# High halves first in three places, and a third gate projection ahead of the state-space outputs

## Chip, core and metric

The kernel runs on one core of a Trainium2 chip. The metric is device time in microseconds, the median of three runs. TensorE (PE) does the matmuls, VectorE (DVE) and ScalarE (ACT) everything elementwise, GpSimd (POOL) and SyncE (SP) little but memory sets and DMA issues.

## What is computed

One layer of a bidirectional hybrid encoder on 1024 tokens of width 1024, in float32. Three mixers (a state-space model S5, a gated linear recurrence RG-LRU, a gated linear attention GLA) work on slices of one projection; each is projected up, multiplied by its gate and added; a mixing matrix, a residual and a mixture of 16 experts follow.

```python
def reference(x, ...):
    h = x
    xn = rms_norm(h, mix_norm_g)
    p = xn @ w_in
    y_s5 = s5_mixer(p[..., OFF_S5:OFF_LRU], ...)
    y_lru = rg_lru_mixer(p[..., OFF_LRU:OFF_Q], ...)
    y_gla = gla_mixer(p[..., OFF_Q:OFF_K], p[..., OFF_K:OFF_V], ...)
    gates = jax.nn.sigmoid(p[..., OFF_GATE:].reshape(bsz, seq, N_BRANCH, D_MODEL))
    merged = (gates[:, :, 0] * (y_s5 @ w_up_s5)
              + gates[:, :, 1] * (y_lru @ w_up_lru)
              + gates[:, :, 2] * (y_gla @ w_up_gla))
    h = h + merged @ w_mix_out
    h = h + ec_ffn(rms_norm(h, ffn_norm_g), w_router, w_exp_gate, w_exp_up, w_exp_down)
    return rms_norm(h, final_norm_g)

def rg_lru_direction(xc, w_a, b_a, w_x, b_x, lam, reverse):
    xr = xc.reshape(bsz, seq, LRU_BLOCKS, LRU_BLOCK)
    r = jax.nn.sigmoid(jnp.einsum('bsnc,ncd->bsnd', xr, w_a).reshape(bsz, seq, LRU_WIDTH) + b_a)
    i = jax.nn.sigmoid(jnp.einsum('bsnc,ncd->bsnd', xr, w_x).reshape(bsz, seq, LRU_WIDTH) + b_x)
    log_a = -LRU_C * r * jax.nn.softplus(-lam)
    a = jnp.exp(log_a)
    mult = jnp.sqrt(jnp.maximum(-jnp.expm1(2 * log_a), 0))
    _, h = lax.associative_scan(_lin_combine, (a, mult * (i * xc)), reverse=reverse, axis=1)
    return h
```

## The kernel before

Every float32 product is made of three matmuls. An operand is split into a high half, rounded by a copy on ACT (L54), and a low half, the difference, taken on DVE (L62, or L57 where a scale goes in); a product is then high·low + high·high + low·high, accumulated in one PSUM tile. `mm3` (L67) writes these three in that order, with the low half of its last argument first. `wsplit` loads weights (`wraw`) and splits them into `wh` and `wl`.

All matmuls in question are 128x128 by 128x512. `proj` (matmuls at L386) makes one 128-column block of the input projection from the normalized input (xnH, xnL): 8 chunks x 3 products x 2 halves of the tokens are 48 matmuls into a PSUM tile `pj`, of which there are two. `gate` calls it for a gate block and evacuates with tanh on ACT. `up` (L396) multiplies a mixer's output halves y with a block of its up-projection: 12 matmuls for S5 and GLA, 24 for the LRU. `gated` joins both on DVE and adds to `merged`.

The stages are Python generators. `drive` takes a list of tasks (projections, gates with ups) and a generator, and after every task goes some steps on in the generator; when the tasks are out, the generator runs to its end alone:

```python
    def drive(tasks, gen, n):
        for t in tasks:
            t()
            for _ in range(n):
                next(gen, None)
        for _ in gen:
            pass
```

A scheduler then orders the instructions of each engine, with a preference for what stands in `tc.high_priority()`, and the buffer counts of the pools set how far ahead it can go. Each engine works its own list in order.

Until 272 us the S5 generator runs, with the remaining columns of the projection and two gates of branch 0 (`early_gate`, pool `pgp` of two buffers) as tasks. Then `s5_out(0)` and `s5_out(1)` use these two: gate, up, `gated`. In the GLA stage (to 447 us) the tasks are `s5_out(2)` to `s5_out(7)`, each of which makes its own gate, and `ahead(0)` to `ahead(2)`, three gates for later (`gates_s5`, L849). The generator computes two head pairs: scores (L789), masked on DVE (L795), products with the values (L802, L809), a normalization and eight transposes (L835), and y. In the LRU stage (to 565 us) the tasks are `gla_out` and the gates of its branch. For each of four channels, a convolution gives xc, its halves are xch and xcl (L62), and 24 matmuls (`mm3` in `lru_gen`, L925, profile lines L68 to L70) make the gates r and i in both directions, into `mx` tiles, of which there are four; scans on DVE (L950) follow. The rest of the gates and ups run until 688 us, and then the mixer: eight token tiles, each of 24 matmuls of the halves of merged (MH, ML) with the mixing weights (wmh, wml) into a bank `mo`, of which there are two; `residual` empties it on DVE (H). Experts follow from 835 us on.

Of the kernel before, what the change touches and what calls it, by code (L numbers as in the profile page):

```python
# [20 lines left out]
KT = D // P  # L21
# [21 lines left out]
def hybrid_encoder(ctx: ExitStack, tc: tile.TileContext, A, out, dbg=None):  # L43
# [346 lines left out]
    def up(w, ys, j):  # L390
        wh, wl = wsplit(w[:, j * P:(j + 1) * P], len(ys))
        ps = pj()
        for k, (yh, yl) in enumerate(ys):
            for i, (ww, yy) in enumerate(((wh, yl), (wh, yh), (wl, yh))):
                for h in range(2):
                    te.matmul(ps[:, h], ww[:, k], yy[:, h * 512:(h + 1) * 512],  # L396
                              start=(k == 0 and i == 0), stop=(k == len(ys) - 1 and i == 2))
        return ps
# [64 lines left out]
    def early_gate(j):  # L463
        if not early:
            early[-1] = pgctx.enter_context(tc.tile_pool(name="pgp", bufs=2, side="left", reuse_waits="tile"))
        early[j] = gate(0, j, early[-1])
# [23 lines left out]
    cols_rest += [lambda j=j: evac(proj(O_LRU + j * P), LD[j * P:(j + 1) * P]) for j in range(4)]  # L490
    cols_rest += [lambda j=j: early_gate(j) for j in range(2)]

# [187 lines left out]

    for j in range(2):
        s5_out(j)
# [165 lines left out]

    gates_s5 = [lambda j=j: s5_out(j) for j in range(2, KT)] + [lambda j=j: ahead(j) for j in range(3)]  # L849
    drive(gates_s5, gla_gen(), 10)  # L850
# [60 lines left out]
    def lru_gen():  # L911
        for c in range(4):
# [3 lines left out]
            for d in range(2):  # L916
# [4 lines left out]
                for h in range(2):  # L921
                    hs = slice(h * 512, h * 512 + 512)
                    for i, (o_, hb_) in enumerate(((rr_, hba), (ii_, hbx))):
                        ps = mx()
                        mm3(ps, WGh[:, 2 * d + i], WGl[:, 2 * d + i], xh[:, hs], xl[:, hs], True, True)  # L925
                        act(o_[:, hs], ps, AF.Tanh, bias=hb_[:, q], scale=0.5)
# [160 lines left out]
    PT = psm.tile([P, 2, 512], F32, name="PT", bufs=1)  # L1087

    def mix(t, w, ps, k0, k1):
        for k in range(k0, k1):  # L1090
            mm3(ps, MH[t][:, k], ML[t][:, k], w[0][:, k], w[1][:, k], k == 0, k == KT - 1)
# [25 lines left out]
    for t in range(NT):  # L1117
        ps = bank("mo")
        mix(t, wm[0], ps, 0, 2)
        next(lgen, None)  # L1120
        mix(t, wm[0], ps, 2, 4)
        next(lgen, None)
        mix(t, wm[0], ps, 4, KT)
        residual(t, 0, h0, ps, w0p)
# [563 lines left out]
```

## Time and profile before

| what | us |
| --- | --- |
| median of 3 runs | 1964.01 |
| lowest and highest | 1962.24, 1964.66 |
| profiled run, its time | 1962.37 |
| its span, first to last instruction | 1960.3 |

The granted clock of TensorE, mean over the profiled run, is 0.983. The profile was read in this way: the busy times by stretch, then what PE waits for, then the timeline at the places that the change touches. A row of the timeline is a start, a duration, the engine, the line, what is written from what, a count, and in brackets the idle time of the engine just before with what ended it.

### The profile page before, as it was taken

To read this page: it belongs to the slowest core of one execution; us is meant where nothing else is said; L and a number is where in the kernel's file an instruction comes from. 1 tells how busy PE (TensorE), PEld (TensorE's weight loads), DVE (VectorE), ACT (ScalarE), POOL (GpSimd) and SP (SyncE) were. 2 spreads that over 40 slices of the span, in tenths; PEclk is the share of its full clock that TensorE was granted. 3 is DMA by queue.
4 is the path that set the end of the run, shared out by engine and by line. 5 is a ranking of instruction groups with operands and counts; after the bars stand their busy time and mean duration, and the time that the engine had idled before them with its cause. 6 is when DMAs were issued, how large, how long until landed. Compare 5 with 4: busy or idle time off the path is not lost.

```text
span 1960.3 us, 25359 instructions
## 1 busy us (share of the span) xinstructions
PE 1871.1 (95%) x9502; PEld 1536.3 (78%) x9502; DVE 1499.6 (76%) x1896; ACT 1167.0 (60%) x1381; POOL 150.9 (8%) x207
## 2 busy tenths in 40 slices
PE   7999999999899999489999999999999999999996
PEld 6878866777778878368888888888888888888884
DVE  6467225558874253889999999999999999999987
ACT  5221234435672131357778777777777877777785
POOL 1834000000000001000000000000000000000000
PEclk9999999999999999689999999999999999999998
DMA  5431331302213163779999999999999999999992
GB/s 170 107 101 38 97 98 29 87 25 72 70 34 88 33 225 127 303 284 370 390 386 383 391 379 378 384 389 384 384 390 379 379 383 394 379 383 388 385 356 97
DMA packets 263231, 495.94 MB, mean 253 GB/s; under 512 B 26757, under 2 KB 82469, under 8 KB 263109
## 3 DMA queue, kind: packets, MB, share of 16 engines
q1 hardware_dynamic: 253476, 466.54, 65.3%
q0 software_dynamic: 7184, 25.69, 4.3%
q10 hardware_dynamic: 2448, 2.10, 0.5%
q8 instruction: 74, 1.21, 0.2%
q14 instruction: 49, 0.39, 0.1%
HBM read 464.55 MB, written 29.74 MB: 252 GB/s over the span
## 4 chain that ended last, share of the span: by engine, by line
PE 80%; DVE 6%; ACT 2%; issue 2%; DMA 1%; SPq 0%; POOLq 0%; DVEq 0%; ACTq 0%
PE py L1484 17%; PE pj L386 13%; PE gu L68 12%; PE gu L70 12%; PE gu L69 12%; PE pj L396 3%; PE tp L1441 2%; PE mo L68 2%; PE mo L70 2%; PE mo L69 2%; ACT xwh L54 1%; DVE junk L1342 1%; DVE lr L950 1%; PE mx L809 0%; PE mx L802 0%
## 5 line engine op out<-in xcount | busy, mean ns | idle before, releaser
L239 DVE TENSOR_TENSOR xwl<-rawb,xwh 128x1024 fp32r<-128x1024 f32 x528 | 613.8, 1218 | 40.0 <-ACT xwh L54 39.1
L54 ACT ACTIVATE xwh<-rawb 128x1024 fp32r<-128x1024 f32 x528 | 521.7, 1052 | 14.1 <-PE gu L70 7.4
L68 PE MATMUL gu<-xwl,xeh 128*128 128x512 f32 x1024 | 406.9, 397 | 0.0
L70 PE MATMUL gu<-xwh,xel 128*128 128x512 f32 x1024 | 399.8, 390 | 0.0
L69 PE MATMUL gu<-xwh,xeh 128*128 128x512 f32 x1024 | 399.0, 390 | 0.0
L239 DVE TENSOR_TENSOR xwl<-rawa,xwh 128x1024 fp32r<-128x1024 f32 x192 | 226.1, 1219 | 25.3 <-ACT xwh L54 25.3
L70 PEld LDWEIGHTS gu<-xwh,xel 128*128 128x128 f32 x1024 | 192.4, 188 | 41.5 <-DVE xel L62 0.2
L69 PEld LDWEIGHTS gu<-xwh,xeh 128*128 128x128 f32 x1024 | 192.8, 188 | 37.7
L68 PEld LDWEIGHTS gu<-xwl,xeh 128*128 128x128 f32 x1024 | 192.7, 188 | 37.3 <-ACT xeh L54 0.2
L54 ACT ACTIVATE xwh<-rawa 128x1024 fp32r<-128x1024 f32 x192 | 192.9, 1052 | 7.1 <-PE py L1484 7.1
L386 PE MATMUL pj<-xnL,wh 128*128 128x512 f32 x576 | 181.6, 394 | 3.9 <-ACT ev L54 2.2
L386 PE MATMUL pj<-xnH,wl 128*128 128x512 f32 x576 | 180.6, 393 | 0.0
L386 PE MATMUL pj<-xnH,wh 128*128 128x512 f32 x576 | 180.2, 392 | 0.0
L1484 PE MATMUL py<-xwl,hTh 128*128 128x512 f32 x512 | 159.2, 392 | 3.6 <-DVE xwl L239 3.6
L1484 PE MATMUL py<-xwh,hTl 128*128 128x512 f32 x512 | 158.0, 390 | 0.5 <-DVE hTl L62 0.5
L1484 PE MATMUL py<-xwh,hTh 128*128 128x512 f32 x512 | 157.8, 389 | 0.0
L54 ACT ACTIVATE wh<-wraw 128x1024 fp32r<-128x1024 f32 (+2 forms) x60 | 49.4, 827 | 176.8 <-PE pj L386 117.0
L62 DVE TENSOR_TENSOR wl<-wraw,wh 128x1024 fp32r<-128x1024 f32 (+2 forms) x60 | 57.6, 961 | 106.8 <-ACT wh L54 96.8
L386 PEld LDWEIGHTS pj<-xnL,wh 128*128 128x128 f32 x576 | 107.1, 188 | 30.4 <-ACT ev L54 3.7
L386 PEld LDWEIGHTS pj<-xnH,wh 128*128 128x128 f32 x576 | 107.9, 188 | 24.7 <-issue 2.0
L386 PEld LDWEIGHTS pj<-xnH,wl 128*128 128x128 f32 x576 | 107.2, 188 | 25.3 <-issue 1.9
L54 ACT ACTIVATE hTh<-tp 128x512 fp32r<-128x512 f32 x64 | 38.4, 599 | 125.3 <-PE tp L1441 125.3
(474 smaller groups left out, 2523.2 us busy)
## 6 DMA issues: line engine op xcount, KB each, us to landing
rawb<-in_w_exp_down_dram SPq DMA_DIRECT2D x90, 1024.0 KB, 8.8
rawb<-in_w_exp_up_dram SPq DMA_DIRECT2D x88, 1024.0 KB, 8.1
rawb<-in_w_exp_gate_dram SPq DMA_DIRECT2D x86, 1024.0 KB, 8.3
rawa<-in_w_exp_up_dram SPq DMA_DIRECT2D x40, 1024.0 KB
rawa<-in_w_exp_gate_dram SPq DMA_DIRECT2D x33, 1024.0 KB
rawa<-in_w_exp_down_dram SPq DMA_DIRECT2D x23, 1024.0 KB
wraw<-in_w_in_dram SPq DMA_DIRECT2D x36, 512.0 KB, 4.3
rawc<-in_w_exp_down_dram SPq DMA_DIRECT2D x15, 1024.0 KB
```

Of the source, the lines that this page charges most:

```text
L54: return s.activation(o, i, f, bias=bias, scale=scale, **k)
L62: (eng or v).tensor_tensor(lo, src, h.bitcast(F32), SUB)
L68: te.matmul(ps, lh, rl, start=first, stop=False)
L69: te.matmul(ps, lh, rh, start=False, stop=False)
L70: te.matmul(ps, ll, rh, start=False, stop=last)
L239: e.tensor_tensor(o, a, b, op)
L386: te.matmul(ps[:, h], w[:, k], xx[:, k, h * 512:(h + 1) * 512], start=(k == 0 and i == 0), stop=(k == KT - 1 and i == 2))
L396: te.matmul(ps[:, h], ww[:, k], yy[:, h * 512:(h + 1) * 512], start=(k == 0 and i == 0), stop=(k == len(ys) - 1 and i == 2))
L950: v.tensor_tensor_scan(rv(hh[d]), rv(hh[d]), rv(gi[d]), initial=0.0, op0=MUL, op1=ADD)
L1342: v.tensor_scalar(junk[:, half_], PT[:, half_], cand.bitcast(F32), 0.0, op0=OP.is_ge, op1=ADD, accum_out=cnt)
L1441: te.transpose(ps[:, j * P:(j + 1) * P], src[:, j * P:(j + 1) * P], idn)
L1484: te.matmul(E.py[:, h], a[:, j], b[:, h * 512:(h + 1) * 512], start=(f == 0 and j == 0 and p_ == 0), stop=(f == 3 and j == 3 and p_ == 2))
```

## The change

Four things. `up` takes the products with the high halves of all y first, then those with the low halves. `early_gate` makes three gates instead of two, with a third buffer, `s5_out(2)` moves in front of the GLA stage with it, and `gates_s5` has one task fewer. The LRU gates take WGh·xh and WGl·xh before WGh·xl. The first mixer tile takes its 16 products with MH before the 8 with ML, without the steps of `logits` in between (there are none at that point).

```diff
     def up(w, ys, j):
         wh, wl = wsplit(w[:, j * P:(j + 1) * P], len(ys))
         ps = pj()
-        for k, (yh, yl) in enumerate(ys):
-            for i, (ww, yy) in enumerate(((wh, yl), (wh, yh), (wl, yh))):
-                for h in range(2):
-                    te.matmul(ps[:, h], ww[:, k], yy[:, h * 512:(h + 1) * 512],
-                              start=(k == 0 and i == 0), stop=(k == len(ys) - 1 and i == 2))
+        terms = [(w_, k, y[0]) for k, y in enumerate(ys) for w_ in (wh, wl)] + [(wh, k, y[1]) for k, y in enumerate(ys)]
+        for i, (ww, k, yy) in enumerate(terms):
+            for h in range(2):
+                te.matmul(ps[:, h], ww[:, k], yy[:, h * 512:(h + 1) * 512], start=(i == 0), stop=(i == len(terms) - 1))
         return ps
...
-            early[-1] = pgctx.enter_context(tc.tile_pool(name="pgp", bufs=2, side="left", reuse_waits="tile"))
+            early[-1] = pgctx.enter_context(tc.tile_pool(name="pgp", bufs=3, side="left", reuse_waits="tile"))
...
-    cols_rest += [lambda j=j: early_gate(j) for j in range(2)]
+    cols_rest += [lambda j=j: early_gate(j) for j in range(3)]
...
-    for j in range(2):
+    for j in range(3):
         s5_out(j)
     pgctx.close()
...
-    gates_s5 = [lambda j=j: s5_out(j) for j in range(2, KT)] + [lambda j=j: ahead(j) for j in range(3)]
+    gates_s5 = [lambda j=j: s5_out(j) for j in range(3, KT)] + [lambda j=j: ahead(j) for j in range(3)]
     drive(gates_s5, gla_gen(), 10)
...
                         ps = mx()
-                        mm3(ps, WGh[:, 2 * d + i], WGl[:, 2 * d + i], xh[:, hs], xl[:, hs], True, True)
+                        gate_ = 2 * d + i
+                        for n, (w_, x_) in enumerate(((WGh, xh), (WGl, xh), (WGh, xl))):
+                            te.matmul(ps, w_[:, gate_], x_[:, hs], start=(n == 0), stop=(n == 2))
...
+    def mix_low_last(t, w, ps):
+        for k in range(KT):
+            te.matmul(ps, MH[t][:, k], w[0][:, k], start=(k == 0), stop=False)
+            te.matmul(ps, MH[t][:, k], w[1][:, k], start=False, stop=False)
+        for k in range(KT):
+            te.matmul(ps, ML[t][:, k], w[0][:, k], start=False, stop=(k == KT - 1))
+
...
-        mix(t, wm[0], ps, 0, 2)
-        next(lgen, None)
-        mix(t, wm[0], ps, 2, 4)
-        next(lgen, None)
-        mix(t, wm[0], ps, 4, KT)
+        if t:
+            mix(t, wm[0], ps, 0, 2)
+            next(lgen, None)
+            mix(t, wm[0], ps, 2, 4)
+            next(lgen, None)
+            mix(t, wm[0], ps, 4, KT)
+        else:
+            mix_low_last(t, wm[0], ps)
```

In the three places below, L386 rows are gate matmuls and L396 rows ups. Lines of the changed kernel are one lower around them, apart from L926, the LRU gates.

First PE at the end of the S5 stage, between the last products of its output gate (Z,wg) and the first up. Before:

```order
L386 MATMUL pj<-xnL,wh 128x512 x2
L644 MATMUL mx<-Z,wg 128x512 x8
L386 MATMUL pj<-xnH,wh 128x512 x2
L386 MATMUL pj<-xnH,wl 128x512 x2
L396 MATMUL pj<-y,wh 128x512 x4
L396 MATMUL pj<-y,wl 128x512 x2
```

and now:

```order
L643 MATMUL mx<-Z,wg 128x512 x8
L386 MATMUL pj<-xnH,wh 128x512
L386 MATMUL pj<-xnH,wl 128x512 x2
L386 MATMUL pj<-xnL,wh 128x512 x2
...
L386 MATMUL pj<-xnH,wh 128x512 x2
L386 MATMUL pj<-xnH,wl 128x512 x2
L396 MATMUL pj<-y,wh 128x512 x2
L396 MATMUL pj<-y,wl 128x512 x2
L396 MATMUL pj<-y,wh 128x512 x2
```

Four gate matmuls stood there, and 45 stand there now.

Second, PE at the end of the GLA stage, from the last scores of the second head pair to its transposes (idn,gt) and the first up of y. Before, the scores and the filling behind them:

```order
L789 MATMUL mx<-gin 128x128 x2
L386 MATMUL pj<-xnH,wl 128x512
L386 MATMUL pj<-xnL,wh 128x512 x2
L386 MATMUL pj<-xnH,wh 128x512 x2
L386 MATMUL pj<-xnH,wl 128x512
L802 MATMUL mx<-gt,sc 128x64
```

and further on, around the transposes:

```order
L386 MATMUL pj<-xnL,wh 128x512 x2
L386 MATMUL pj<-xnH,wh 128x512 x2
L386 MATMUL pj<-xnH,wl 128x512 x2
L835 MATMUL mx<-idn,gt 128x128 x8
L386 MATMUL pj<-xnL,wh 128x512 x2
L386 MATMUL pj<-xnH,wh 128x512 x2
```

and now:

```order
L788 MATMUL mx<-gin 128x128 x2
L801 MATMUL mx<-gt,sc 128x64
L808 MATMUL mx<-gt 64x64 x2
...
L801 MATMUL mx<-gt,sc 128x64 x2
L808 MATMUL mx<-gt 64x64 x4
L808 MATMUL mx<-gt,gin 64x64 x2
L834 MATMUL mx<-idn,gt 128x128 x8
L396 MATMUL pj<-y,wh 128x512 x2
L396 MATMUL pj<-y,wl 128x512 x2
```

No gate matmul stands there any more; before, there were six between the scores and the masked products, 25 between the last products and the transposes and twelve between these and the first up.

Third, PE at the LRU gates of the first channel. Before:

```order
L386 MATMUL pj<-xnH,wl 128x512
L68 MATMUL mx<-xcl,lwh 128x512
L69 MATMUL mx<-xch,lwh 128x512
L70 MATMUL mx<-xch,lwl 128x512
L68 MATMUL mx<-xcl,lwh 128x512
```

and now:

```order
L396 MATMUL pj<-y,wh 128x512
L926 MATMUL mx<-xch,lwh 128x512
L926 MATMUL mx<-xch,lwl 128x512
L926 MATMUL mx<-xch,lwh 128x512
L926 MATMUL mx<-xch,lwl 128x512
L926 MATMUL mx<-xch,lwh 128x512
L926 MATMUL mx<-xcl,lwh 128x512 x2
```

The products with xcl, first before, stand behind those with xch of several tiles now.

## Rows read from the trace of the kernel before

**Rows 1.** The head of the page.

```profile
span 1960.3 us, 25359 instructions
```

**Rows 2.** Busy time by stretch: PE, PEld, DVE, ACT, POOL, granted clock, DMA share, GB/s.

```profile
447.00:565.00 118.00, 109.55 (x464) 86.87 (x463) 101.27 (x116) 75.43 (x94) 0.54 (x8) 0.99 0.25 68
565.00:688.00 123.00, 123.00 (x543) 101.72 (x542) 48.83 (x47) 40.91 (x49) 1.04 (x11) 1.00 0.18 52
...
835.00:1940.00 1105.00, 1093.78 (x5108) 905.17 (x5108) 1011.94 (x994) 861.81 (x956) 43.19 (x33) 0.99 0.99 370
```

**Rows 3.** PE's waits to 800 us: total us, times, longest.

```profile
PE mx L68 <- DVE xcl L62: 5.5, 3, 2.5
...
PE pj L396 <- DVE y L57: 3.3, 2, 2.1
...
PE mo L70 <- DVE ML L57: 2.0, 1, 2.0
```

**Rows 4.** Timeline of PE at the S5 ups.

```profile
254.82 5.74 PE L644 MATMUL mx<-Z,wg 128*128 128x512 f32 x13
...
263.61 2.07 PE L396 MATMUL pj<-y,wh 128*128 128x512 f32 x4 [2.13 <-DVE y L57]
...
269.37 1.19 PE L396 MATMUL pj<-y,wh 128*128 128x512 f32 x4 [1.15 <-DVE y L57]
```

**Rows 5.** Timeline of PE in a gate, the first and the last of seven consecutive pairs.

```profile
239.03 0.61 PE L386 MATMUL pj<-xnH,wl 128*128 128x512 f32 x2
...
241.75 0.61 PE L386 MATMUL pj<-xnH,wl 128*128 128x512 f32 x2
```

**Rows 6.** Short stretches behind PE waits, columns as in rows 2.

```profile
263.50:266.50 3.00, 2.89 (x7) 2.31 (x8) 1.52 (x3) 1.38 (x1) 0.00 (x0) 0.52 0.19 49
266.50:269.30 2.80, 1.72 (x7) 1.06 (x5) 2.07 (x1) 0.70 (x1) 0.00 (x0) 0.90 0.00 0
528.60:531.60 3.00, 2.93 (x9) 2.36 (x10) 3.00 (x4) 1.82 (x3) 0.00 (x0) 0.71 0.00 0
531.60:534.00 2.40, 2.40 (x8) 1.88 (x7) 2.40 (x4) 1.81 (x4) 0.00 (x0) 0.65 0.30 51
690.80:694.00 3.20, 3.15 (x14) 2.57 (x15) 3.08 (x11) 2.28 (x4) 0.00 (x0) 1.00 1.05 406
```

**Rows 7.** Timeline at the end of the GLA stage.

```profile
432.25 0.39 PE L789 MATMUL mx<-gin 64*128 64x128 f32 x4
...
434.07 0.33 PE L802 MATMUL mx<-gt,sc 128*128 128x64 f32 x2
...
436.08 0.30 PE L809 MATMUL mx<-gt,gin 64*64 64x64 f32 x4
...
442.76 1.09 PE L835 MATMUL mx<-idn,gt 128*128 128x128 f32 x8 [0.49 <-DVE gt L239]
...
445.40 1.06 ACT L54 ACTIVATE y<-gt 128x1024 fp32r<-128x1024 f32 x1 [6.97 <-DVE gt L57]
...
446.47 1.07 PE L396 MATMUL pj<-y,wh 128*128 128x512 f32 x4
```

**Rows 8.** Timeline at the gates of the second LRU channel, and of the last.

```profile
495.64 1.06 ACT L54 ACTIVATE xch<-xc 128x1024 fp32r<-128x1024 f32 x1 [5.83 <-DVE xc L57]
497.66 1.20 DVE L62 TENSOR_TENSOR xcl<-xc,xch 128x1024 fp32r<-128x1024 f32 x1
...
498.92 0.50 PE L68 MATMUL mx<-xcl,lwh 128*128 128x512 f32 x1 [1.35 <-DVE xcl L62]
...
561.46 0.50 PE L68 MATMUL mx<-xcl,lwh 128*128 128x512 f32 x1 [1.65 <-DVE xcl L62]
```

**Rows 9.** Timeline of the mixer's beginning.

```profile
693.13 8.04 DVE L57 SCALAR_TENSOR_TENSOR ML<-merged,MH 128x1024 fp32r<-128x1024 f32 x7
...
701.08 1.49 DVE L239 TENSOR_TENSOR H<-mo,H 128x512 f32<-128x512 f32 x2
...
702.23 0.48 PE L68 MATMUL mo<-wml,MH 128*128 128x512 f32 x1
```

## The prediction

> **What bounds the kernel now.** I read the page's head first, for the span of 1960.3 us [rows 1], and then the busy times by stretch [rows 2]. From 835 us on, the experts hold TensorE (PE) for 1093.78 of 1105.00 us at a granted clock of 0.99. Nothing of that is touched, so whatever the front part gains or loses should reach the end at full size. In the front two kinds of stretch stand out. From 565 to 688 us PE is busy for 123.00 of 123.00 us: there only the number of matmuls counts. From 447 to 565 us, the RG-LRU stage, PE is busy for 109.55 of 118.00 us and VectorE (DVE) for 101.27: there a chain over DVE, ScalarE (ACT) and PE and the matmuls that fill PE's pauses are nearly equal, so removing a PE wait need not shorten anything.
>
> Next come PE's waits by what ended them, over the first 800 us [rows 3]. Three of the groups are the change's targets: the LRU gates wait 5.5 us for the low half of the convolved input (xcl) in three places, the up projections 3.3 us for a low half of y in two, the mixer 2.0 us for a low half (ML) in one. The timeline of PE then shows where: the S5 up projections after 2.13 us of idle at 263.61 and after 1.15 us at 269.37 [rows 4]. Last I read one stretch in which PE waits hardly at all, the end of the GLA stage [rows 7], because the order of the changed kernel takes the filling work from just there.
>
> **A unit of cost.** Every gate projection is 48 matmuls of 128x512. From the pair at 239.03 us to the pair at 241.75 lie six pairs, twelve matmuls, in 2.72 us [rows 5], which is 0.227 us each. So a gate costs 10.9 us of PE, wherever it stands; the change only moves it.
>
> **The change part by part.**
>
> *The third early gate and the S5 up projections: -5.0 us.* The order of the changed kernel has 45 gate matmuls between the last Z,wg products and the first up, 4 before. The Z,wg group ends near 260.5 us [rows 4], and 45 x 0.227 = 10.2 us of matmuls bring PE to about 270 to 271; the first up then begins with the high half of y, and the last low half is there at about 269.3, as the wait ending at 269.37 says. Both waits go: 2.13 + 1.15 = 3.28 us. There is more: behind the first wait the granted clock was 0.52 for 3.00 us and 0.90 for 2.80 us [rows 6], a loss of 3.00 x 0.48 + 2.80 x 0.10 = 1.7 us against full clock, which goes with it. Bounds: -3.3 (the clock falls elsewhere) to -5.0; I take -5.0, since PE then has matmuls through the whole tail. The high-first order in the ups adds nothing here, since the gate already covers both halves. The gate's own evacuation on ACT and the split of its weights (wh on ACT, wl on DVE) are the same instructions as before, earlier, and the first low half of y, there at 263.6, is wanted only at 270, so some microseconds are to spare.
>
> *The same gate is then missing in the GLA stage: +13.7 us.* The S5 gates are handed out one task at a time between steps of the GLA generator, and now there is one task fewer. In the order of the changed kernel the fillers are used up before the end. Counting gate and up matmuls in both orders: at the first transpose of the second head pair PE has done 1104 of them instead of 1041, that is 63 more (48 of the moved gate and 15 others pulled forward): +63 x 0.227 = +14.3 us. From there to the first GLA up projection the order holds 104 instead of 159, 55 fewer (12.5 us), but does the stretch become shorter? That is the main question, and the timeline answers it [rows 7]. From the last score product at 432.25 us to the masked product at 434.07 PE waits for two masking copies on DVE; the six gate matmuls between only fill that. From the end of the last output products (436.08 + 0.30) on, a chain runs outside PE: ACT squares, then DVE's reduction and reciprocal root, transposes on PE at 442.76, scaling, y on ACT at 445.40, the first up at 446.47. That is 10.1 us, during which PE now does 37 gate matmuls (37 x 0.227 = 8.4 us) and eight transposes (1.1 us). At 442.76 PE had already waited 0.49 us for DVE: the chain ends last there, not the filling. With the filling gone, the chain stays and PE idles: some 9 us at the end and 1.4 us in each of two mask steps, with smaller pieces of 0.5 and 1.1 us, which is about 12 to 13 us, the size of the work that left. What the stretch can lose is only the bit by which fillers held the chain up; at the transposes it is nothing, as the 0.49 us say, and the up at 446.47 starts at y's end (445.40 + 1.06), so again nothing. For the two mask steps, where the chain may have come a matmul's pitch or so later in each, I take -0.6, an estimate. Bounds: -0.6 to -12.5 (all of it, the rival below). So y of GLA is ready 14.3 - 0.6 - 5.0 = 8.7 us later than before.
>
> *The LRU gates, high halves first: +0.2 us.* In the channel at 498.92 us the high half is ready at 496.70 (495.64 + 1.06), the low half at 498.86, and PE waits 1.35 us for that [rows 8]. Now PE can run eight products (four PSUM banks, two products each) ahead of the low half: 8 x 0.227 = 1.8 us of work moved into the wait. But in front of the gates there is also less to do: by y of GLA the changed order has done 1208 gate and up matmuls (1200 before), by the last channel's gates 1569 (1578 before). The wait that remains is for the same instruction of DVE, xcl, which still stands behind the same scans; in the channel with the longest wait, 2.5 us [rows 3], DVE's order is unchanged. Since PE is full from 565 us on [rows 2], the stage's length is told by the last channel's gates and what is left then: 1.8 us less for the products done ahead, 9 matmuls more (2.0 us): +0.2. Bounds: the waits go altogether (-5.5), with them the low clock of 0.71 and 0.65 behind the 2.5 us wait [rows 6] (3.00 x 0.29 + 2.40 x 0.35 = -1.7) and the 8 matmuls done before y (-1.8), in all -9.0; the other end is the 2.0 us for 9 matmuls with nothing gained and one more stretch at the low clock, 1.7 us, in all +3.7. I take +0.2, nearest to the row at 561.46, where after 1.65 us of wait the PE-bound stretch begins.
>
> *The first mixer tile: 0.* It no longer waits 2.0 us. But its result sits in one of two banks (mo), and the tile after next needs that bank. The low halves of the other seven tiles occupy DVE from 693.13 for 8.04 us, and the addition that empties the first bank follows at 701.08; the third tile starts at 702.23 [rows 9]. DVE's order there is as before, so PE arrives 2 us earlier and waits 2 us longer, once. Bounds: -2.0 (other work fits) to +1.7 (the wait lowers the clock as the one of 2.13 us did).
>
> The Trainium skill, "Perfetto Trace Analysis", section "Optimizing Tensor Performance", asks that independent matmul groups rotate through PSUM banks so that one's evacuation overlaps the next group's matmuls. By that rule the tile's wait would be hidden and the gain of 2 us real; the rows speak against it here, since the evacuation stands behind DVE's splits.
>
> **Sum.** -5.0 + 14.3 - 0.6 + 0.2 + 0 = +8.9 us on the profiled run of 1962.37 us: 1971.3 us. The median of the runs is 1964.01, 1.6 us above the profiled run, so the forecast is **1972.9 us**. About 0.2%, or 3.9 us, is what a measurement of this kernel can tell from no change.
>
> **Rivals.**
>
> *The LRU stage pays it back* (0.16). If what bounds 447 to 565 us is PE's idle time and not the DVE chain, the term there is -9.0 instead of +0.2, and the sum -0.3; with the mixer's 2 us, -2.3. That gives 1961.7 to 1963.7 us, no change. For it: PE is busier than DVE there. Against: DVE turns to xcl at 497.66, a microsecond after the high half is there [rows 8], since other work stands ahead of it in its queue, and that work stays.
>
> *Faster: the GLA tail costs nothing* (0.08). If the fillers are what makes the chain late, the stretch shrinks by the whole 12.5 us that leave it. This decides as soon as the chain from 436.38 to 446.47 can run in what PE still has there, 1.1 us of transposes; the sum is then -5.0 + 14.3 - 12.5 + 0.2 = -3.0, and with the LRU term -12.2: 1951.8 to 1961.0 us. Against it stands the 0.49 us wait, and that no PE filler lies between most of the chain's steps.
>
> *The clock falls in each new pause* (0.15). Behind idles of 2.13 and 2.5 us the granted clock fell; after the mixer's 2.0 us it stayed at 1.00 [rows 3, 6]. The changed kernel has pauses of 6 and 3 us around the GLA transposes and perhaps one in the LRU stage and one in the mixer. At 1.7 us each, three of them give 1978.0 us. The Trainium skill, "TensorE: Matmul & The Clock Gate", section "HAM oscillation — how this bites in real kernels", describes this, a cold restart behind waits between bursts; the trace agrees at 0.52 and 0.71. I keep it as a rival because behind the GLA tail DVE's chain covers part of the slower matmuls.
>
> **How the numbers follow.** Forecast 0.61, the LRU stage pays back 0.16, faster tail 0.08, low clock 0.15. The forecast's own range is 1968 to 1977. The range reaches down over most of the first rival and up to the third: 1962.5 to 1978.0. Faster by over 0.2%: 0.08. Within 0.2%: 0.17, the first rival and a little of the forecast's lower edge, less what of the second rival falls there. Slower by over 0.2%: 0.75.
>
> **What would show it.** In the profile after: no PE wait ahead of the S5 ups, and full clock there; PE waits of about 6 and 3 us on either side of the second head pair's transposes and of 1.4 us before the last masked products; y of GLA about 8.7 us later; waits for xcl still there or replaced; a PE wait of about 2 us before the third mixer tile. If y of GLA is not later, the step on the filling is wrong; if it is later but the mixer begins on time, the LRU term is.

## The result: 0.7% slower

| kernel | median us | runs | lowest, highest | profiled run | its span |
| --- | --- | --- | --- | --- | --- |
| before | 1964.08 | 4 | 1962.24, 1964.66 | 1962.37 | 1960.3 |
| changed | 1978.09 | 4 | 1975.83, 1980.02 | 1980.02 | 1977.9 |

The ratio of after to before is 1.0068, 95% interval 1.0055 to 1.0081: 14.0 us slower between the medians, where the forecast was 8.9 slower. The median lies 0.1 us above the stated range, 1962.5 to 1978.0 us (the forecast's own part of it was 1968 to 1977). The four runs of the changed kernel stand in two pairs, near 1976 and near 1980; the profiled one is of the upper pair, 17.6 us above the profiled run of before.

PE's waits over the first 860 us, as in [rows 3] (total us, times, longest):

```profile
PE mx L834 <- DVE gt L239: 6.6, 2, 6.4
...
PE pj L386 <- ACT wh L54: 3.6, 2, 2.0
PE mx L801 <- DVE sc L794: 3.2, 5, 1.2
...
PE pt L1105 <- DVE H L239: 2.0, 1, 2.0
PE pj L396 <- ACT y L54: 1.9, 1, 1.9
...
PE mx L926 <- ACT xch L54: 1.7, 1, 1.7
PE mx L926 <- DVE xcl L62: 1.3, 1, 1.3
```

The wait of the S5 ups for y and the mixer's wait for ML are gone from the list, and the LRU gates wait 3.0 us in two places instead of 5.5 in three (a new wait of 2.0 us for split weights, wh, also lies in the LRU stage). In their place stand a wait of 6.4 us ahead of the second head pair's transposes (L834), 1.9 us ahead of the first GLA up, 1.2 us ahead of masked products (L801) and 2.0 us in the mixer (L1105). The changed kernel's timeline of PE at the places that [rows 4] and [rows 7] to [rows 9] show of before:

```profile
272.22 0.62 PE L396 MATMUL pj<-y,wh 128*128 128x512 f32 x2
...
371.70 1.06 PE L834 MATMUL mx<-idn,gt 128*128 128x128 f32 x8 [0.20 <-DVE gt L239]
...
432.82 0.43 PE L801 MATMUL mx<-gt,sc 128*128 128x64 f32 x2 [0.16 <-DVE sc L794]
...
439.26 0.69 PE L801 MATMUL mx<-gt,sc 128*128 128x64 f32 x2 [1.19 <-DVE sc L794]
...
446.68 0.69 PE L801 MATMUL mx<-gt,sc 128*128 128x64 f32 x2 [1.19 <-DVE sc L794]
...
457.31 1.97 PE L834 MATMUL mx<-idn,gt 128*128 128x128 f32 x8 [6.39 <-DVE gt L239]
461.21 1.22 PE L396 MATMUL pj<-y,wh 128*128 128x512 f32 x2 [1.93 <-ACT y L54]
...
574.38 0.39 PE L926 MATMUL mx<-xch,lwh 128*128 128x512 f32 x1
...
703.08 0.39 PE L1092 MATMUL mo<-wmh,MH 128*128 128x512 f32 x1
...
716.66 0.66 PE L1105 MATMUL pt<-idn,H 128*128 128x128 f32 x4 [2.01 <-DVE H L239]
717.08 0.48 PE L68 MATMUL mo<-wml,MH 128*128 128x512 f32 x1
...
860.69 1.73 PE L1452 MATMUL tp<-idn,xe 128*128 128x128 f32 x7 [6.11 <-DMA xe<-HN,idx]
```

Two more rows of before are needed beside [rows 4] and [rows 7] to [rows 9], the first head pair's transposes and the first expert's:

```profile
363.79 1.06 PE L835 MATMUL mx<-idn,gt 128*128 128x128 f32 x8 [0.18 <-DVE gt L239]
...
842.94 1.30 PE L1441 MATMUL tp<-idn,xe 128*128 128x128 f32 x5 [6.28 <-DMA xe<-HN,idx]
```

From these rows (the mixer of before began at 688.24) follows where the time went:

| point on PE | before | after | later by | change since the point above |
| --- | --- | --- | --- | --- |
| first pair's transposes | 363.79 | 371.70 | 7.9 | +7.9 |
| second pair's transposes | 442.76 | 457.31 | 14.6 | +6.6 |
| first GLA up | 446.47 | 461.21 | 14.7 | +0.2 |
| last LRU channel's gates | 561.46 | 574.38 | 12.9 | -1.8 |
| mixer | 688.24 | 703.08 | 14.8 | +1.9 |
| first expert | 842.94 | 860.69 | 17.8 | +2.9 |

So there are three things to explain: 7.9 us in front of the GLA chain, 6.6 us inside it, and 2.9 us in the mixer. The last two do not fit the prediction. One pair of profiles is not exact to a microsecond, though: two kernels below with the instructions of before up to the first pair's transposes (mixer only, LRU order only) have these at 365.63 and 365.58 instead of 363.79.

The granted clock tells of the last two; the busy times of short stretches in the changed kernel (columns as in [rows 2]):

```profile
430.00:435.00 5.00, 4.84 (x56) 3.62 (x55) 1.92 (x6) 0.00 (x0) 0.00 (x0) 0.92 0.09 27
435.00:440.00 5.00, 3.81 (x39) 3.17 (x40) 1.43 (x4) 0.00 (x0) 0.00 (x0) 0.50 0.00 0
440.00:445.00 5.00, 5.00 (x52) 4.41 (x54) 0.00 (x0) 0.00 (x0) 0.00 (x0) 0.50 0.00 0
...
717.00:720.00 3.00, 3.00 (x13) 2.36 (x11) 2.82 (x25) 3.00 (x7) 1.30 (x2) 0.59 1.04 382
720.00:724.00 4.00, 4.00 (x16) 3.53 (x15) 2.60 (x3) 1.06 (x2) 0.00 (x0) 0.50 1.04 403
724.00:728.00 4.00, 4.00 (x22) 3.43 (x21) 0.00 (x0) 1.06 (x1) 0.00 (x0) 0.95 1.04 386
```

In the GLA tail the clock is 0.50, that is 1.2 GHz instead of 2.4, and stays there although PE is busy for all of 440 to 445 us. It fell at about 434.2 us, as 0.92 over five microseconds is 0.8 us at 0.50: ahead of the first wait of 1.19 us, and with one of 0.16 us between 430 and 435. In the mixer it falls behind the 2.01 us wait that replaced the one for ML.

### The profile page after: what moved, and what is told of

It is laid out like the page before. It is cut to its first block, busy times and chain, and to the rows that moved or that the text cites. A ratio compares the mean times of both kernels' runs of the same rounds, so it can differ in the third digit from the quotient of the medians.

```text
span 1977.9 us, 25356 instructions
## 1 busy us (share of the span) xinstructions
PE 1881.6 (95%) x9502; PEld 1547.5 (78%) x9502; DVE 1501.1 (76%) x1896; ACT 1170.2 (59%) x1383; POOL 150.9 (8%) x207
## 4 chain that ended last, share of the span: by engine, by line
PE 79%; DVE 7%; ACT 3%; issue 2%; DMA 1%; POOL 0%; POOLq 0%; DVEq 0%; ACTq 0%
PE py L1495 17%; PE gu L68 12%; PE gu L70 11%; PE gu L69 11%; PE pj L386 11%; PE pj L396 4%; PE tp L1452 2%; PE mo L68 1%; PE mo L69 1%; PE mo L70 1%; PE mx L926 1%; ACT gt L54 1%; ACT xwh L54 1%; DVE junk L1353 1%; PE mx L801 1%
## 5 line engine op out<-in xcount | busy, mean ns | idle before, releaser
L54 ACT ACTIVATE xwh<-rawb 128x1024 fp32r<-128x1024 f32 x528 | 521.7, 1052 | 13.4 <-PE gu L70 6.8
L386 PE MATMUL pj<-xnL,wh 128*128 128x512 f32 x576 | 182.5, 396 | 6.5 <-ACT wh L54 3.6
L386 PE MATMUL pj<-xnH,wh 128*128 128x512 f32 x576 | 181.3, 394 | 0.0
L386 PE MATMUL pj<-xnH,wl 128*128 128x512 f32 x576 | 180.6, 393 | 0.7 <-DVE wl L62 0.7
L386 PEld LDWEIGHTS pj<-xnL,wh 128*128 128x128 f32 x576 | 108.0, 189 | 34.4 <-ACT wh L54 5.2
L386 PEld LDWEIGHTS pj<-xnH,wl 128*128 128x128 f32 x576 | 108.2, 189 | 25.2 <-DVE wl L62 1.6
L386 PEld LDWEIGHTS pj<-xnH,wh 128*128 128x128 f32 x576 | 108.7, 189 | 24.5 <-issue 1.8
```

Source lines behind the costliest of these rows:

```text
L54: return s.activation(o, i, f, bias=bias, scale=scale, **k)
L386: te.matmul(ps[:, h], w[:, k], xx[:, k, h * 512:(h + 1) * 512], start=(k == 0 and i == 0), stop=(k == KT - 1 and i == 2))
```

## The experiments

Each is compared with runs of the kernel before on the same chip. My theory after the result, called A in the expectations: the gate's place makes the loss, the low clock adds to it in the GLA tail and in the mixer, and the high-first orders do little. Times of the runs with a ratio against before and its 95% interval (microseconds given with a verdict in the text are the ratio's share of 1964 us):

| run | median us | before, us | ratio | interval |
| --- | --- | --- | --- | --- |
| third gate only | 1970.94 | 1965.69 | 1.0035 | 1.0022 to 1.0048 |
| up and LRU orders only | 1968.56 | 1965.69 | 1.0019 | 1.0010 to 1.0028 |
| mixer only | 1965.13 | 1965.69 | 1.0005 | 0.9994 to 1.0015 |
| all but the mixer | 1975.33 | 1965.69 | 1.0059 | 1.0042 to 1.0076 |
| third gate, its up back in GLA | 1965.30 | 1964.39 | 1.0007 | 0.9998 to 1.0016 |
| an LRU gate instead | 1956.82 | 1964.39 | 0.9964 | 0.9952 to 0.9976 |
| order for the fill | 1990.05 | 1964.39 | 1.0133 | 1.0117 to 1.0148 |
| fill with idle products | 1986.19 | 1964.39 | 1.0107 | 1.0082 to 1.0131 |
| up order only | 1961.27 | 1964.42 | 0.9984 | 0.9976 to 0.9993 |
| LRU order only | 1968.08 | 1964.42 | 1.0025 | 1.0012 to 1.0037 |
| two LRU gates | 1958.94 | 1964.42 | 0.9971 | 0.9961 to 0.9981 |
| an LRU gate and the up order | 1955.96 | 1964.83 | 0.9949 | 0.9935 to 0.9964 |

### The parts of the change, apart

The third early gate alone, with all products in the old order:

```diff
-name="pgp", bufs=2
+name="pgp", bufs=3
...
-    cols_rest += [lambda j=j: early_gate(j) for j in range(2)]
+    cols_rest += [lambda j=j: early_gate(j) for j in range(3)]
...
-    for j in range(2):
+    for j in range(3):
         s5_out(j)
...
-    gates_s5 = [lambda j=j: s5_out(j) for j in range(2, KT)] + [lambda j=j: ahead(j) for j in range(3)]
+    gates_s5 = [lambda j=j: s5_out(j) for j in range(3, KT)] + [lambda j=j: ahead(j) for j in range(3)]
```

> Only the third early gate (three buffers, s5_out(2) ahead of the GLA stage); all products in the order of the kernel before. Theory A (the gate's place makes the loss: it stands ahead of the start of the GLA chain and is then missing as filling, and the low clock in the unfilled tail adds some 6 us): first GLA up at about 461 us as with the whole change, the mixer's wait for ML back, 10 to 13 us slower than before. Rival B (the gate pays 5 us and the high-first orders lose): about 5 us faster than before. No wait for y at the S5 ups by A and B.

It is 0.35% slower (6.9 us). Rival B falls: the gate does not pay, even alone. The 10 to 13 us of theory A are too much, though. In the GLA tail PE waits at the same places as in the whole change; its timeline of PE:

```profile
436.96 0.43 PE L802 MATMUL mx<-gt,sc 128*128 128x64 f32 x2 [0.76 <-DVE sc L795]
...
441.77 0.43 PE L802 MATMUL mx<-gt,sc 128*128 128x64 f32 x2 [1.19 <-DVE sc L795]
...
451.16 1.97 PE L835 MATMUL mx<-idn,gt 128*128 128x128 f32 x8 [6.38 <-DVE gt L239]
456.32 1.22 PE L396 MATMUL pj<-y,wh 128*128 128x512 f32 x2 [3.19 <-DVE y L57]
```

with the high half of y on ACT, and the clock:

```profile
453.95 1.06 ACT L54 ACTIVATE y<-gt 128x1024 fp32r<-128x1024 f32 x1 [7.13 <-DVE gt L57]
```

```profile
435.00:440.00 5.00, 4.25 (x65) 3.40 (x65) 1.44 (x4) 0.00 (x0) 0.00 (x0) 1.00 0.00 0
440.00:445.00 5.00, 3.59 (x48) 2.82 (x44) 1.44 (x4) 0.21 (x1) 0.00 (x0) 0.86 0.33 108
```

The first GLA up comes at 456.32, not at 461: the mask steps ran at full clock here, and the clock fell only in the last masked products. The step from 436.96 to 441.77 us takes 4.8 us, where the same step of the whole change takes 7.4 (439.26 to 446.68). From 436.96 here and 439.26 there to the first up, the order of the matmuls is the same in both. In the old order this up wants the low half of y; the high half is ready at 455.01 (453.95 + 1.06), 8.5 us later than before (446.46, [rows 7]), and in the whole change, where the first up starts with it, it is 14.7 us later.

The orders of the ups and the LRU gates, without the third gate and the mixer's part; against the changed kernel:

```diff
-name="pgp", bufs=3
+name="pgp", bufs=2
...
-    for j in range(3):
+    for j in range(2):
         s5_out(j)
...
-        if t:
-            mix(t, wm[0], ps, 0, 2)
...
-        else:
-            mix_low_last(t, wm[0], ps)
+        mix(t, wm[0], ps, 0, 2)
```

> Only high halves first in the up projections and the LRU gates; two early gates, mixer as before. Theory A: the S5 wait shrinks by under 1 us, the LRU stage keeps its length since the DVE chain sets it: within 2 us of before, either way. Rival B (these orders lose): 5 us or more slower. Rival C (the LRU waits of 5.5 us come off): 5 to 9 us faster.

It is 0.19% slower (3.7 us), so theory A's 2 us are missed, and rival C falls; rival B's 5 us are not reached, though the interval (2.0 to 5.5 us) takes them in. What each order does alone is told below. At the S5 ups a wait of 2.5 us remains, now for the second y's high half:

```profile
266.80 1.22 PE L396 MATMUL pj<-y,wh 128*128 128x512 f32 x2 [2.53 <-ACT y L54]
```

Taking the first y's low half later only brings PE to the next late operand.

The first mixer tile alone; against the kernel before:

```diff
+        if t:
             mix(t, wm[0], ps, 0, 2)
...
+        else:
+            mix_low_last(t, wm[0], ps)
```

> Only the first mixer tile takes its products with ML last. Theory A: the 2 us wait for ML becomes a wait of about 2 us for the first bank's evacuation before the third tile, and the granted clock falls behind it to between 0.5 and 0.6 for some microseconds: about 3 us slower. The prediction's step: 0, the wait only moved. Rival (the wait is really hidden): 2 us faster.

No difference can be measured (1.0005). The prediction's step holds here, and theory A does not; its timeline of PE and the busy time behind:

```profile
704.62 0.66 PE L1104 MATMUL pt<-idn,H 128*128 128x128 f32 x4 [2.02 <-DVE H L239]
705.03 0.48 PE L68 MATMUL mo<-wml,MH 128*128 128x512 f32 x1
```

```profile
705.00:708.00 3.00, 3.00 (x22) 2.54 (x21) 2.83 (x25) 3.00 (x7) 1.25 (x2) 1.00 1.05 384
```

The wait of 1.98 us for ML has become one of 2.02 us for H, that is for the addition that empties the first bank, and the clock stayed at 1.00 behind it. In the profile of the whole change the same wait, 2.01 us long, was followed by 0.59 and 0.50. The same code can go either way.

The low clock is not peculiar to the new order either. Of the four profiles that have it, the clock fell behind this wait in two (the whole change, and the fill below), with 157.6 and 157.7 us from the mixer's first matmul to the first expert, and stayed in two (mixer only, order for the fill), with 154.5 and 154.6. Of the ten with the old order it fell behind the wait of 1.9 to 2.0 us for ML in three (up and LRU orders, 0.56 from 695 to 698 us; third gate with its up back in GLA, 0.56 from 693 to 696; two LRU gates, 0.52 from 685 to 688), with 155.9 to 156.3 us, against 154.5 to 155.0 in the other seven. So it is not shown that the mixer's part brings the low clock.

The whole change without its mixer part; against the changed kernel:

```diff
-        else:
-            mix_low_last(t, wm[0], ps)
```

> The whole change without its mixer part. Theory A: about 3 us faster than the whole change, so 11 us slower than before, with the profile at full clock behind the mixer's first tile. The prediction's step: the same as the whole change, 14 us slower.

1.0059 against 1.0068 for the whole change, with overlapping intervals: whether the mixer's part costs anything on the average can't be told from these. But this kernel has the same instructions as the whole change up to the mixer, and its profile shows the GLA tail at another clock:

```profile
431.86 0.43 PE L801 MATMUL mx<-gt,sc 128*128 128x64 f32 x2 [0.16 <-DVE sc L794]
...
436.67 0.43 PE L801 MATMUL mx<-gt,sc 128*128 128x64 f32 x2 [1.19 <-DVE sc L794]
...
442.04 0.69 PE L801 MATMUL mx<-gt,sc 128*128 128x64 f32 x2 [1.18 <-DVE sc L794]
...
452.66 1.97 PE L834 MATMUL mx<-idn,gt 128*128 128x128 f32 x8 [6.38 <-DVE gt L239]
456.56 1.22 PE L396 MATMUL pj<-y,wh 128*128 128x512 f32 x2 [1.93 <-ACT y L54]
```

```profile
430.00:435.00 5.00, 4.84 (x80) 3.93 (x81) 1.43 (x4) 0.00 (x0) 0.00 (x0) 1.00 0.02 3
435.00:440.00 5.00, 3.81 (x60) 3.22 (x58) 1.43 (x4) 0.00 (x0) 0.00 (x0) 0.96 0.00 0
440.00:445.00 5.00, 3.82 (x31) 3.06 (x29) 1.43 (x4) 0.00 (x0) 0.00 (x0) 0.50 0.29 108
```

The clock fell here about 440 us, in the whole change before 435. From the masked products at 431.86 to the first up (456.56) it takes 24.7 us, and in the whole change from the same products (432.82) 28.4. That is one pair of profiled runs of like instructions, and the clearest sign that the clock is a term of its own.

Run alone, the gate costs 6.9 us, the two orders 3.7 and the mixer's part 1.0, which can't be told from nothing: 11.6 us together, where the ratio of the whole change gives 13.4 (10.8 to 15.9).

### Where the gate's loss comes from

The third gate again, but kept in an evacuation buffer, so that s5_out(2) with its up can be the GLA stage's first task again; only the 48 gate matmuls stand ahead of the S5 outputs:

```diff
-        early[j] = gate(0, j, early[-1])
+        early[j] = gate(0, j, early[-1] if j < 2 else None)
...
-    cols_rest += [lambda j=j: early_gate(j) for j in range(2)]
+    cols_rest += [lambda j=j: early_gate(j) for j in range(3)]
```

> As the gate-only kernel, but only the gate itself stands ahead of the S5 outputs (kept in one of the two evacuation buffers); its up projection and s5_out(2) are again the first task of the GLA stage. Theory A1 (the GLA chain begins late because all of s5_out(2) stands ahead of it): the first GLA projection (alr) some 5 us earlier than in the gate-only kernel, y of GLA near 449, 5 us faster than the gate-only kernel, so within 2 us of before. Theory A2 (what costs is only that the filling is missing at the end, wherever the gate stands): y near 456 as in the gate-only kernel, 7 us slower than before.

The time is that of before (1.0007), 5 us less than with the gate only, as theory A1 said. The first product of the GLA chain (alr) in this kernel:

```profile
288.77 1.12 PE L733 MATMUL mx<-alr,wal 16*128 16x512 f32 x2
...
445.55 1.97 PE L835 MATMUL mx<-idn,gt 128*128 128x128 f32 x8 [6.38 <-DVE gt L239]
```

and in the kernel with the gate only:

```profile
293.49 1.12 PE L733 MATMUL mx<-alr,wal 16*128 16x512 f32 x2
```

Before, it stood at 286.45. So the chain starts 7.0 us late where all of s5_out(2) is in front, 2.3 us late where only its gate is. The waits of 6.38 us ahead of the transposes and of 3.19 us ahead of the first up are in both. The mask steps differ: from 420 us on PE waits 2.3 us for masked scores with the gate only, and 0.3 us here, where the GLA stage has one task more to hand out and six matmuls of an up still stand ahead of the last masked products. By the second pair's transposes PE has done the same number of gate and up matmuls in both kernels, and it is there 5.6 us earlier here. So what the late start costs and what the shorter filling costs are not told apart by this pair. The gate alone, even so, gains nothing: what it saves at the S5 tail comes back as idle time in the GLA tail.

Then another gate in the same place: the last of the LRU branch, which before stood directly ahead of the mixer, with its tanh written to memory and read back there. The GLA stage keeps all its filling.

```diff
+    def early_lru():
+        ps = proj(O_GATE + D + 7 * P)
+        with tc.high_priority():
+            ev = xw.tile([P, S], F32, name="ev", bufs=2)
+            act(ev, ps.rearrange("p a b -> p (a b)"), AF.Tanh, scale=0.5)
+            dma(G7D, ev)
...
-    cols_rest += [lambda j=j: early_gate(j) for j in range(2)]
+    cols_rest += [lambda j=j: early_gate(j) for j in range(2)] + [early_lru]
...
```

> Another gate in the same place: two S5 gates ahead as before, and behind them the LRU branch's gate of block 7, which the kernel before makes last, ahead of the mixer; its tanh goes to memory and is loaded again there. All products in the order of before, the GLA stage keeps all its filling. If the S5 tail's waits are worth 5 us and the loss comes from the GLA stage's missing filling: 48 matmuls (10.9 us) more before GLA, of which about 5 are free, and 10.9 us less behind the LRU stage: 4 to 6 us faster than before. Rival (any gate there delays the chains by its whole length): no change, within 2 us.

It is 0.36% faster (7.1 us), a little more than the 4 to 6 expected. The GLA tail is as before, with the same short wait:

```profile
447.21 1.09 PE L844 MATMUL mx<-idn,gt 128*128 128x128 f32 x8 [0.49 <-DVE gt L239]
450.90 1.07 PE L396 MATMUL pj<-y,wh 128*128 128x512 f32 x4
```

The first up is 4.4 us later than before (446.47), since 48 more matmuls (10.9 us) stand in front and the S5 tail gives 6.5 us of them back; the mixer then begins at 682.51 instead of 688.24, because those 48 no longer stand behind the LRU stage. Two such gates instead of one:

```diff
-[lambda j=j: early_gate(j) for j in range(2)] + [early_lru]
+[lambda j=j: early_gate(j) for j in range(2)] + [lambda j=j: early_lru(j) for j in (7, 6)]
...
```

> Two gates of the LRU branch, blocks 7 and 6, ahead of the S5 outputs and through memory, instead of one. If a gate there pays only as far as PE idled (the first fills the 5 us), the second moves 10.9 us from behind the LRU stage to ahead of the GLA chain and changes nothing: within 1.5 us of the kernel with one gate, 5 to 8 us faster than before. Rival (the early gates pay by themselves): some 7 us faster again.

The ratio is 0.9971, not to be told from that of one gate (0.9964). The second gate finds no idle time ahead of GLA and only changes its place.

### The clock in the GLA tail

To see the clock apart from the chain, I filled the tail with matmuls that compute nothing. First the order for it, the whole change with 6 generator steps per task instead of 10:

```diff
-    drive(gates_s5, gla_gen(), 10)
+    drive(gates_s5, gla_gen(), 6)
```

> Reference for the next kernel: the whole change with 6 instead of 10 generator steps per task in the GLA stage, so that all tasks are out before the last score products. No filling is left from the first masked products of the second head pair on. Theory A: y of GLA at about 457 to 462, granted clock 0.5 in the tail, about as slow as the whole change, 10 to 15 us slower than before.

and then the fill, 54 matmuls into a PSUM tile that nobody reads, held back by a small product of the masked scores (fill(6) in three mask steps, fill(26) behind the last output products, fill(10) behind the transposes):

```diff
+    def fill(n, vN):
+        ps = pj()
+        te.matmul(ps[:, 0, 0:64], sc[:, 0, 0], vN[:, 0, 0:64], start=True, stop=True)
+        for i in range(n):
+            te.matmul(ps[:, i % 2], xnH[:, 0, 0:P], xnH[:, i // 2 % KT, i % 2 * 512:i % 2 * 512 + 512],
+                      start=(i < 2), stop=(i >= n - 2))
...
```

> The kernel for the fill (6 steps per task) plus 54 matmuls of 128x512 into a PSUM tile that nobody reads, made to depend on the masked scores so that they stand in the tail: 18 in the mask steps, 26 ahead of the last transposes, 10 behind. They add 12 us of PE work that computes nothing. Theory A (the chain sets the tail's length and the low clock adds to it): clock 1.00 in the tail, y 3 to 8 us earlier than in the kernel without them, and the program as much faster or at least not slower. Rival (PE's work sets the tail's length): y and the program up to 12 us later.

Both are slower than the whole change (1.0133 and 1.0107), the first by more than was expected: fewer steps per task put more filling ahead of the GLA chain. As a test of the program's time the pair is not clean, since the clock had fallen to about 0.65 between 420 and 430 us in both, ahead of the fill, and the two LRU orders differ. What can be compared is the last piece, from the last masked products to the first up. Without the fill, at 0.50 throughout:

```profile
457.61 0.69 PE L801 MATMUL mx<-gt,sc 128*128 128x64 f32 x2 [1.19 <-DVE sc L794]
...
468.22 1.97 PE L834 MATMUL mx<-idn,gt 128*128 128x128 f32 x8 [6.38 <-DVE gt L239]
472.31 1.22 PE L396 MATMUL pj<-y,wh 128*128 128x512 f32 x2 [2.13 <-ACT y L54]
```

With it, at full clock:

```profile
462.37 0.33 PE L810 MATMUL mx<-gt,sc 128*128 128x64 f32 x2
...
471.00 1.04 PE L845 MATMUL mx<-idn,gt 128*128 128x128 f32 x8
474.40 0.62 PE L396 MATMUL pj<-y,wh 128*128 128x512 f32 x2
```

```profile
458.00:465.00 7.00, 7.00 (x93) 5.95 (x93) 1.46 (x4) 0.18 (x1) 0.00 (x0) 1.00 0.22 77
```

The piece takes 14.7 us without the fill and 12.0 with it, although 36 matmuls (8.2 us at full clock) were added; before, with real gates in it, it took 12.4 (434.07 to 446.47, [rows 7]). The fill costs nothing there, as a chain outside PE says it should, and the low clock costs 2.7 us. The expectation for the whole tail was missed, though: y comes 2.1 us later than without the fill (474.40 against 472.31), where 3 to 8 us earlier was expected. Until about 457 us PE was at half the clock in both, and there the first twelve products of the fill held the chain up: from 436.81 to 456.94 the two mask steps and the products before them take 20.1 us, and 13.9 without the fill (436.30 to 450.18).

### The two orders, apart

Only the ups with high halves first, and only the LRU gates; against the kernel before, the one or the other of:

```diff
-        for k, (yh, yl) in enumerate(ys):
-            for i, (ww, yy) in enumerate(((wh, yl), (wh, yh), (wl, yh))):
...
+        terms = [(w_, k, y[0]) for k, y in enumerate(ys) for w_ in (wh, wl)] + [(wh, k, y[1]) for k, y in enumerate(ys)]
...
-                        mm3(ps, WGh[:, 2 * d + i], WGl[:, 2 * d + i], xh[:, hs], xl[:, hs], True, True)
...
+                        for n, (w_, x_) in enumerate(((WGh, xh), (WGl, xh), (WGh, xl))):
...
```

> Only the up projections take high halves first. In the kernel with both orders the S5 up still waited (2.5 us for the second y's high half and smaller waits), so no gain is expected at the S5 tail. If the 3.7 us lost by the two orders together come from the ups: 2 to 4 us slower; if they come from the LRU gates: within 1.5 us of before.

> Only the LRU gates take high halves first. The gates of the last channel then stand ahead of 10 gate and up matmuls that stood before them (1600 instead of 1610 counted to there), so 2.3 us more are left behind them. Theory (the stage's time is set by what is left behind the last channel's gates): 1 to 3 us slower than before. Rival of the prediction (the waits of 5.5 us come off): 5 us faster. Rival (the ups carry the loss): within 1 us.

The ups' order is 0.16% faster (3.1 us), the LRU gates' 0.25% slower (4.9). For the ups no expectation had a gain; for the LRU gates the theory holds in sign, with more than its 1 to 3 us. Both show in one place, the start of the last channel's gates and of the mixer. With the ups' order the channel's row is

```profile
570.34 0.50 PE L68 MATMUL mx<-xcl,lwh 128*128 128x512 f32 x1 [2.29 <-DVE xcl L62]
```

and with the LRU gates' order

```profile
563.19 0.39 PE L927 MATMUL mx<-xch,lwh 128*128 128x512 f32 x1
```

Counted from each kernel's first GLA up (446.47 before, 448.67, 448.25), these gates start after 115.0 us before, 121.7 with the ups' order and 114.9 with the gates'. With the ups' order 43 more matmuls of gates and ups stand in front of them than before, with the gates' order ten fewer, as the orders of PE's instructions tell. 43 more in front cost 6.7 us there and save 43 x 0.227 = 9.8 behind: 3.0 us. Ten fewer in front save nothing there, since the chain is as long as before, and cost 2.3 us behind, with 0.7 us of wait for xcl: 3.1 us. For scale, the mixer-only kernel, with the instructions of before in this stage, has 115.9 us in front and 126.8 behind, where before has 115.0 and 126.8. The low halves are still waited for; only the place changes.

Last, the two parts that gained, together (the two diffs above, of `early_lru` and of `up`):

> The LRU gate of block 7 ahead of the S5 outputs (through memory) together with high halves first in the ups; two S5 gates, LRU gates and mixer as before. The first alone gave 7.1 us, the second alone 3.2 us, in different stages (the S5 tail, and the work left behind the last LRU channel's gates). If they are independent: 9 to 11 us faster than before. Rival (the order of the ups changes the LRU stage's interleaving differently here): no faster than the LRU gate alone.

It has a ratio of 0.9949, 10.0 us faster than before (8.9 between the medians), the best of all runs; its mixer begins at 682.39 us. Its interval (0.9935 to 0.9964) overlaps that of the LRU gate alone (0.9952 to 0.9976), so that the second part adds to the first is likely and not shown.

## Why the prediction came out as it did

*The direction and its reason were right.* The gate fills the S5 tail and empties the GLA tail. In the profile after, PE's waits stand where the prediction put them: 1.2 us in each of two mask steps (1.4 forecast), 6.4 us ahead of the transposes (about 6), 1.9 behind (about 3; with the gate only, where the first up wants the low half, it is 3.2).

*The S5 tail, -5.0.* Measured: the first pair's transposes are 7.9 us later, with 60 more matmuls in front of them (13.6 us), so 5.7 us came back. The forecast of -5.0 is a little short.

*The gate missing in GLA, +13.7.* The term was mis-sized. The prediction has y of GLA 8.7 us later. Three profiles with the gate moved show what was left out. Where the clock fell only in the last masked products (gate only), the high half of y is 8.5 us later; where it fell at about 440 us (all but the mixer), the first up, which starts with that half, is 10.1 us later; where it fell at about 434 (the whole change), 14.7. So PE's idle time and the chain were costed rightly at full clock, and the excess goes with the low clock: the step took the durations of [rows 7], and in the unfilled tail PE ran at 0.50. At full clock a mask step takes 4.8 us (gate only, 436.96 to 441.77; 5.0 before, 429.08 to 434.07) and the last piece 12.0; in the whole change two mask steps take 6.4 and 7.4, and the last piece, from the last masked products to the first up, 14.5. That is 6.7 us more, and 6.0 is what was missing. The third rival named such a loss, at 1.7 us for each pause, in the wrong form: it put the loss behind long pauses, on matmuls of 128x512, while in this tail the clock fell ahead of the first 1.2 us wait, and what became slower were the chain's own small matmuls. That this rival's 1978.0 us is almost the measured median is luck.

The step also said that the chain stays and PE idles once the filling is gone. The kernel with the up moved back agrees: it keeps filling in the mask steps and has no low clock there, has the same two waits at the end, and its first up is 4.2 us later than before (450.71). At the mixer that is 1.0 us (689.26 against 688.24), as twelve more gate and up matmuls are done by that first up. The matmuls that the step counted ahead of the chain hold the up of s5_out(2) beside its gate; with the up there the chain starts later and the filling ends sooner, and the gate-only kernel has its first up 5.6 us later than this one.

*The LRU gates, +0.2.* From the first GLA up to the mixer it is 241.8 us before and 241.9 after, so the sum was right. Its parts were not: the order of the LRU gates alone costs 4.9 us and that of the ups gains 3.1, and the prediction gave the ups nothing here and the gates 1.8 us for products done ahead. The table has -1.8 us up to the last channel's gates, but that these products bring it is not shown: the LRU order alone leaves the stretch at 114.9 us (115.0 before), and in the whole change 17 fewer gate and up matmuls stand in it. PE's waits in it are 7.8 us in all and were 8.4, since others came as those for xcl shrank. The count of matmuls left behind the last channel, 9 more, was the right view (+1.9 us there, 2.0 forecast). The rival in which the LRU waits come off falls with the run of the LRU order alone.

*The mixer, 0 with a bound of +1.7.* Half right. The wait moved as described, to within 0.04 us. In the profiled run of the whole change the clock fell behind it and the stretch to the experts took 2.9 us more, beyond the bound; in the run with the mixer's part alone it did not, and three profiles with the old order have such a fall too.

*The two places of the Trainium skill.* By the Trainium skill's rule in "Perfetto Trace Analysis", section "Optimizing Tensor Performance", that matmul groups rotate through PSUM banks so that one's evacuation overlaps the next one's matmuls, the mixer's wait would have been hidden. The mixer-only run differs, with 2.02 us of wait for the evacuation: with two banks, the evacuation stands behind other work of DVE.

The Trainium skill's "TensorE: Matmul & The Clock Gate", section "HAM oscillation — how this bites in real kernels", has waits between bursts send the array back to the lower clock. The trace of the whole change agrees in the mixer (0.59 behind 2.01 us) and not in the GLA tail, where the clock fell ahead of the waits. The rival that rests on this got 0.15, too little for a chain whose own steps are on PE.

## What to carry to other kernels

Work that fills PE's pauses is worth what it saves where the pause was, less what is late because it stands in front of a chain: take it from the stretch where PE is always busy (here behind the LRU stage), not from another stage's filling. Taking filling away from a chain with small matmuls in it can cost more than the idle time, when the clock falls and the chain's own matmuls become slower, as in the whole change. And an operand that comes late is not overtaken by using it last, if all that stands behind still wants the result.

## Of the hardware, not expected

In the whole change the granted clock fell to 0.50 at about 434.2 us, in a stretch of matmuls of 64x64, 64x128 and 128x64 with few of 128x512 between them, while PE was busy for 4.84 of 5 us and waited 0.16 us; before, with gate matmuls between such products, it was 1.00 there. And it did not return while PE was then busy for 5.00 of 5 us with such small matmuls; it rose again during the ups of 128x512 that begin at 461.21 us. Like instructions meet it at different places from run to run: the same tail began to be slow at 434 us in one profile and at 440 in another, and a wait of 2.0 us in the mixer was followed by 1.00 in some and by 0.5 to 0.6 in others. That fits the two pairs of times of the changed kernel, 4 us apart; only one of the four was profiled, so that it is the cause is not shown. With the old mixer the six runs lie as far apart (1971.78 to 1979.75), so the mixer's part alone does not make the pairs.
